# A grouped softmax over 285 MB: tiles of 384 rows for 256, a maximum ahead only within a tile, rows at a tile's ends scaled in halves

## The chip, the cores and the metric

One core of a Trainium2 chip. The metric is the device time of one execution, in microseconds; runs are repeated and the median is quoted.

## The reference, cut to what matters

```python
x: float32 [4, 4096, 4352]                 # 16384 rows of 17,408 bytes
x_g = x.reshape(B, N, 8, 544)              # eight groups in each row
x_g = x_g - x_g.max(axis=-1, keepdims=True)
exp = np.exp(x_g)
out = exp / exp.sum(axis=-1, keepdims=True)
```

285 MB come in and 285 MB go out. "A row" below means 128 rows of x, one on each partition: 2.2 MB, 128 such rows in all.

## The kernel before: the parts that matter

A ring of six buffers, each holding R = 2 rows per partition. SyncE issues the loads, each when the store that used its buffer is complete; GpSimd issues the stores (SyncE the last two). A load or a store is one transfer. In the trace it has 128 packets of R x 17,408 bytes (7936 of 34,816 bytes for GpSimd's 62 stores) and lands in 16 parts, so eight packets a part; a part is taken below for the share of one of the core's 16 DMA engines.

```python
# SyncE: loads
for t in range(nt):
    if t >= NT:
        nc.sync.wait_ge(stored[t % NT], 16 * (t // NT))
    nc.sync.dma_start(out=tile_in[:, :], in_=xt[t]).then_inc(landed[t % NT], 16)
    # ... the last tile is loaded row by row
# VectorE: one maximum ahead, all through
vector_max(0)
for s in range(S):
    vector_max(s + 1)     # waits for the next tile's load where s + 1 begins a tile
    vector_scale(s)       # reciprocal of the sums (waits for exp), then one multiply of 4352
# ScalarE: eight exps a row, one per group, each with its sum; the last one signals
```

Of the kernel before, what the change touches and what calls it, by code (L numbers as in the profile page):

```python
# [1 line left out]

# [5 lines left out]


@with_exitstack  # L10
def kernel(
    ctx: ExitStack,
    tc: tile.TileContext,
    x: bass.AP,
    out: bass.AP,
):
    nc = tc.nc
    G = 8
    P = 128
    R = 2  # L20
    NT = 6
    S = R * NT
    xf = x.flatten_outer_dims()
    of = out.flatten_outer_dims()
    N, D = xf.shape
    Dg = D // G
    nt = N // (P * R)
    nr = nt * R
    turns = (nr - 1) // S
    LAST = 2  # L30
    ring_turns = (nt - LAST) // NT
    steps = ring_turns * NT
    f32 = mybir.dt.float32
    X = mybir.AxisListType.X
    Exp = mybir.ActivationFunctionType.Exp
    xt = xf.rearrange("(t p r) d -> t p (r d)", p=P, r=R)
    ot = of.rearrange("(t p r) d -> t p (r d)", p=P, r=R)
    turn_out = of[:steps * P * R, :].rearrange("(u b p r) d -> u b p (r d)", b=NT, p=P, r=R)

    landed = [tc.alloc_semaphore(f"landed{b}") for b in range(NT)]  # L40
    stored = [tc.alloc_semaphore(f"stored{b}") for b in range(NT)]

    max_done = tc.alloc_semaphore("max_done")
    exp_done = tc.alloc_semaphore("exp_done")
    rec_done = tc.alloc_semaphore("rec_done")
    scaled = tc.alloc_semaphore("scaled")
    last_landed = tc.alloc_semaphore("last_landed")
    last_scaled = tc.alloc_semaphore("last_scaled")
    last_stored = tc.alloc_semaphore("last_stored")

    ctx.enter_context(tc.tile_critical(no_gpsimd_drain=True))  # L51
    bufs = [ctx.enter_context(nc.sbuf_tensor(f"xt{b}", [P, R * D], f32)) for b in range(NT)]
    mx = ctx.enter_context(nc.sbuf_tensor("mx", [P, S, G], f32))
    sm = ctx.enter_context(nc.sbuf_tensor("sm", [P, S, G], f32))
    rs = ctx.enter_context(nc.sbuf_tensor("rs", [P, S, G], f32))

    def take(engine, sem, n=1):
        engine.sem_inc(sem, -n).wait_op(sem, n, "sem-ge")  # L58

    def row(s):  # L60
        b, r = divmod(s, R)
        return bufs[b][:, r * D:(r + 1) * D].rearrange("p (g d) -> p g d", g=G)

    def vector_max(n):
        s = n % S
        i = nc.vector.reduce_max(out=mx[:, s, :], in_=row(s), axis=X, negate=True)  # L66
        if n == nr - 1:
            i.wait_op(last_landed, 16, "sem-ge")
        elif s % R == 0:
            i.wait_op(landed[s // R], 16, "sem-ge")  # L70
        i.then_inc(max_done, 1)

    def vector_scale(n):
        s = n % S
        nc.vector.reciprocal(out=rs[:, s, :], in_=sm[:, s, :]).wait_op(  # L75
            exp_done, s + 1, "sem-ge").then_inc(rec_done, 1)
        xr = row(s)
        nc.vector.tensor_tensor(  # L78
            out=xr,
            in0=xr,  # L80
            in1=rs[:, s, :].unsqueeze(2).to_broadcast([P, G, Dg]),
            op=mybir.AluOpType.mult,
        ).wait_op(rec_done, s + 1, "sem-ge").then_inc(
            scaled if n < (nt - LAST) * R else last_scaled, 1)

    def scalar_exp(s):
        xr = row(s)
        for g in range(G):
            i = nc.scalar.activation(  # L89
                out=xr[:, g, :],  # L90
                in_=xr[:, g, :],
                func=Exp,
                bias=mx[:, s, g:g + 1],
                scale=1.0,
                accum_out=sm[:, s, g:g + 1],
            )
            if g == 0:
                i.wait_op(max_done, s + 1, "sem-ge")
        i.then_inc(exp_done, 1)



    for t in range(nt):
        if t >= NT:
            nc.sync.wait_ge(stored[t % NT], 16 * (t // NT))
        tile_in = bufs[t % NT]
        if t < nt - 1:
            nc.sync.dma_start(out=tile_in[:, :], in_=xt[t]).then_inc(landed[t % NT], 16)  # L108
        else:
            for r in range(R):  # L110
                nc.sync.dma_start(
                    out=tile_in[:, r * D:(r + 1) * D], in_=xt[t, :, r * D:(r + 1) * D],
                ).then_inc(landed[t % NT] if r < R - 1 else last_landed, 16)
    for k in range(LAST):
        t = nt - LAST + k
        nc.sync.wait_ge(last_scaled, (k + 1) * R)
        nc.sync.dma_start(out=ot[t], in_=bufs[t % NT][:, :]).then_inc(last_stored, 16)
    nc.sync.wait_ge(last_stored, 16 * LAST)


    def store(t, target):
        take(nc.gpsimd, scaled, R)
        nc.gpsimd.dma_start(out=target, in_=bufs[t % NT][:, :]).then_inc(stored[t % NT], 16)  # L123

    with nc.gpsimd.Fori(0, ring_turns) as u:
        for t in range(NT):
            store(t, turn_out[u, t])
    for t in range(steps, nt - LAST):
        store(t, ot[t])
    for t in range(nt - NT, nt - LAST):  # L130
        nc.gpsimd.wait_ge(stored[t % NT], 16 * (t // NT + 1))
    nc.gpsimd.drain()

    nc.scalar.preload_act_table(Exp)  # L134
    with nc.Fori(0, turns, engines=OrderedEngineSet([nc.scalar.engine]),
                 head_slot={nc.scalar.engine: 0}):
        for s in range(S):
            scalar_exp(s)
        nc.scalar.sem_inc(max_done, -S)
    for n in range(turns * S, nr):  # L140
        scalar_exp(n % S)


    vector_max(0)
    with nc.vector.Fori(0, turns):
        for s in range(S):
            if s == S - 1:
                for b in range(NT):
                    nc.vector.sem_inc(landed[b], -16)
            vector_max(s + 1)  # L150
            vector_scale(s)
        nc.vector.sem_inc(exp_done, -S)
        nc.vector.sem_inc(rec_done, -S)
    for n in range(turns * S, nr):
        if n + 1 < nr:
            vector_max(n + 1)
        vector_scale(n)


# [1 line left out]
_INS = ['x']  # L161
_OUTS = [((4, 4096, 4352), 'float32')]


# [23 lines left out]
```

## Time and profile before

| | kernel before |
|---|---|
| median | 1327.84 us (1326.93 to 1328.22 over 4 runs) |
| span of the profile | 1326.6 us |
| VectorE busy | 1207.7 us, 91% |
| moved by DMA | 570.47 MB, 430 GB/s over the span |

Read it from the bottom up. 91% for VectorE looks like a bound, but the row of the DMA engines is full in every slice but the last, and the rate does not follow what the engines do: 433 GB/s from 4 to 40 us with VectorE busy for 24.2 of 36 us, and 433 from 330 to 1200 us with it busy for 797 of 870. The prediction below shows those lines. One view is worth reading with suspicion: the chain of waits puts 66% of the span on "another core or an unknown queue". Only one core runs, and SyncE's own waits name what it waited for (columns: us in total, times, longest):

```profile
SPq L108 <- DMA out_dram<-xt: 1213.4, 58, 62.2
```

SyncE is waiting for stores to free buffers nearly all the time: the DMA engines are what there is too little of.

### The profile page before, as it was taken

Reading aid. Unit: us, or ns where it says so; the run is one execution under the profiler, and the core shown is the slowest. Engines: PE = TensorE matmul, PEld = TensorE weight load, DVE = VectorE, ACT = ScalarE, POOL = GpSimd, SP = SyncE. Lnnn points to the kernel's source line nnn. Section 1 sums busy time; section 2 is a strip of 40 time slices with the busy share of each in tenths; the row PEclk is TensorE's granted clock in tenths of the full one; section 3 lists DMA queues with packets and bytes.
Section 4 is the critical chain, followed back from the end, with each engine's and each line's share of the span. In section 5 each row is a group of like instructions: output and inputs, shape, how many; then the busy total and the mean of one; then the engine's idle time right before and its main releaser. Section 6 shows DMA issues by size and latency. Waiting matters only on the chain.

```text
span 1326.6 us, 2968 instructions
## 1 busy us (share of the span) xinstructions
DVE 1207.7 (91%) x384; ACT 764.5 (58%) x2049; POOL 33.3 (3%) x66
## 2 busy tenths in 40 slices
DVE  5999999999889898898998989989889898898984
ACT  3666665656555565555655556556565565555661
POOL 0000000000000000000000000000000000000000
DMA  9999999999999999999999999999999999999998
GB/s 404 420 436 430 429 435 436 436 429 431 435 435 436 430 430 435 436 436 429 431 435 435 436 430 431 434 436 436 429 431 435 435 436 431 429 435 436 431 433 351
DMA packets 18581, 570.47 MB, mean 430 GB/s; under 512 B 2064, under 2 KB 2064, under 8 KB 2064
## 3 DMA queue, kind: packets, MB, share of 16 engines
q1 hardware_dynamic: 9648, 294.13, 51.5%
q0 software_dynamic: 8928, 276.30, 48.2%
q14 instruction: 5, 0.04, 0.0%
HBM read 285.21 MB, written 285.21 MB: 430 GB/s over the span
## 4 chain that ended last, share of the span: by engine, by line
another core or an unknown queue 66%; DMA 7%; DVE 3%; SPq 1%; ACT 0%; issue 0%; POOLq 0%
DMA out_dram<-xt 4%; DMA xt<-in_x_dram 3%; DVE xt L78 1%; DVE mx L66 1%; SPq L108 1%; ACT xt L89 0%; DVE rs L75 0%; POOLq L123 0%
## 5 line engine op out<-in xcount | busy, mean ns | idle before, releaser
L89 ACT ACTIVATE xt<-xt,mx 128x544 f32<-128x544 f32 x1024 | 751.3, 735 | 539.5 <-DVE mx L66 539.5
L66 DVE TENSOR_REDUCE mx<-xt 128x8 f32<-128x4352 f32 x128 | 599.1, 4681 | 95.3 <-DMA xt<-in_x_dram 95.3
L78 DVE TENSOR_TENSOR xt<-xt,rs 128x4352 f32<-128x4352 f32 x128 | 600.6, 4692 | 4.4
L89 ACT ACTIVATION_READ_ACCUMULATOR xt<-xt,mx 128x1 f32 x1024 | 191.2, 187 | 0.0
L123 POOL DMA_DIRECT2D out_dram<-xt x62 | 33.1, 533 | 1240.3 <-POOLq L58 1240.3
L75 DVE RECIPROCAL rs<-sm 128x8 f32<-128x8 f32 x128 | 24.7, 193 | 2.6 <-ACT xt L89 2.6
L134 ACT ACT_TABLE_LOAD x1 | 1.3, 1283 | 1.0 <-SPq L51 1.0
L172 POOL MEMSET const-float32-0.0<- 128x1 f32 x1 | 0.1, 98 | 0.4 <-issue 0.4
L172 POOL MEMSET const-bfloat16-1.0<- 128x1 bf16 x1 | 0.1, 101 | 0.0
L172 POOL MEMSET const-uint8-127<- 128x1 uint8 x1 | 0.1, 99 | 0.0
L172 POOL MEMSET const-float32-1.0<- 128x1 f32 x1 | 0.1, 98 | 0.0
## 6 DMA issues: line engine op xcount, KB each, us to landing
xt<-in_x_dram SPq DMA_DIRECT2D x63, 4352.0 KB, 41.1
out_dram<-xt POOLq DMA_DIRECT2D x62, 4352.0 KB, 51.5
out_dram<-xt SPq DMA_DIRECT2D x2, 4352.0 KB, 19.3
xt<-in_x_dram SPq DMA_DIRECT2D x2, 2176.0 KB, 43.5
```

The costliest lines, as they stand in the source:

```text
L66: i = nc.vector.reduce_max(out=mx[:, s, :], in_=row(s), axis=X, negate=True)
L75: nc.vector.reciprocal(out=rs[:, s, :], in_=sm[:, s, :]).wait_op(exp_done, s + 1, "sem-ge").then_inc(rec_done, 1)
L78: nc.vector.tensor_tensor(out=xr, in0=xr, in1=rs[:, s, :].unsqueeze(2).to_broadcast([P, G, Dg]), op=mybir.AluOpType.mult,).wait_op(rec_don ...
L89: i = nc.scalar.activation(out=xr[:, g, :], in_=xr[:, g, :], func=Exp, bias=mx[:, s, g:g + 1], scale=1.0, accum_out=sm[:, s, g:g + 1],)
L108: nc.sync.dma_start(out=tile_in[:, :], in_=xt[t]).then_inc(landed[t % NT], 16)
L123: nc.gpsimd.dma_start(out=target, in_=bufs[t % NT][:, :]).then_inc(stored[t % NT], 16)
L134: nc.scalar.preload_act_table(Exp)
L172: nc = _bacc.Bacc("TRN2", target_bir_lowering=False, num_devices=1)
```

## The change

Its intent: larger packets, fewer transfers, an earlier start, and a VectorE that finishes a tile, and so releases its store, without first waiting for the next load. To do that it keeps one maximum ahead inside a tile (two maxima stand before the first scaling, as before) but takes none of the next tile before a tile's last scaling. It scales a tile's first and last row in halves, so that the first multiply of such a row needs only half of its exps. The first tile is loaded row by row. 128 rows do not divide by 3, so the last tile has two rows. Cut to its core:

```diff
-    R = 2
-    NT = 6
+    R = 3
+    NT = 4
...
+    def vector_tile(t):
+        n = t * R
+        if sizes[t] == R:
+            vector_max(n)
+            for r in range(R):
+                if r + 1 < R:
+                    vector_max(n + r + 1)
+                vector_scale(n + r, 1 if 0 < r < R - 1 else H)   # H = 2 parts
+        else:                                                     # the last tile, two rows
+            for r in range(sizes[t]):
+                vector_max(n + r)
+                vector_scale(n + r, H)
...
-        i.then_inc(exp_done, 1)
+            if (g + 1) % Gh == 0:          # after four and after eight exps
+                i.then_inc(exp_done, 1)
...
-            vector_max(s + 1)
-            vector_scale(s)
+            vector_tile(t)
```

More of the change, by code (lines that the diff above doesn't have):

```diff
@@ L26 @@
     Dg = D // G
-    nt = N // (P * R)
-    nr = nt * R
-    turns = (nr - 1) // S
+    nr = N // P
+    sizes = nr // R * [R]
+    if nr % R:
+        sizes.append(nr % R)
+    nt = len(sizes)
+    turns = (nt - 1) // NT
+    H = 2
+    Gh = G // H
     LAST = 2
@@ L35, with tile_of @@
     Exp = mybir.ActivationFunctionType.Exp
-    xt = xf.rearrange("(t p r) d -> t p (r d)", p=P, r=R)
-    ot = of.rearrange("(t p r) d -> t p (r d)", p=P, r=R)
+    def tile_of(af, t):
+        lo = t * P * R
+        return af[lo:lo + P * sizes[t], :].rearrange("(p r) d -> p (r d)", p=P)
     turn_out = of[:steps * P * R, :].rearrange("(u b p r) d -> u b p (r d)", b=NT, p=P, r=R)
@@ L46 @@
     scaled = tc.alloc_semaphore("scaled")
-    last_landed = tc.alloc_semaphore("last_landed")
+    first_landed = [tc.alloc_semaphore(f"first_landed{r}") for r in range(1, R)]
+    last_landed = [tc.alloc_semaphore(f"last_landed{r}") for r in range(1, sizes[-1])]
     last_scaled = tc.alloc_semaphore("last_scaled")
@@ L66, in vector_max, with vector_scale @@
         i = nc.vector.reduce_max(out=mx[:, s, :], in_=row(s), axis=X, negate=True)
-        if n == nr - 1:
-            i.wait_op(last_landed, 16, "sem-ge")
-        elif s % R == 0:
+        r = n % R
+        if r == 0:
             i.wait_op(landed[s // R], 16, "sem-ge")
+        elif n < R:
+            i.wait_op(first_landed[r - 1], 16, "sem-ge")
+        elif n // R == nt - 1:
+            i.wait_op(last_landed[r - 1], 16, "sem-ge")
         i.then_inc(max_done, 1)
-    def vector_scale(n):
+    recs = 0
+    def vector_scale(n, parts):
+        nonlocal recs
         s = n % S
-        nc.vector.reciprocal(out=rs[:, s, :], in_=sm[:, s, :]).wait_op(
-            exp_done, s + 1, "sem-ge").then_inc(rec_done, 1)
-        xr = row(s)
-        nc.vector.tensor_tensor(
-            out=xr,
-            in0=xr,
-            in1=rs[:, s, :].unsqueeze(2).to_broadcast([P, G, Dg]),
-            op=mybir.AluOpType.mult,
-        ).wait_op(rec_done, s + 1, "sem-ge").then_inc(
-            scaled if n < (nt - LAST) * R else last_scaled, 1)
+        for k in range(parts):
+            g = slice(k * G // parts, (k + 1) * G // parts)
+            nc.vector.reciprocal(out=rs[:, s, g], in_=sm[:, s, g]).wait_op(
+                exp_done, H * s + (k + 1) * H // parts, "sem-ge").then_inc(rec_done, 1)
+            recs += 1
+            xr = row(s)[:, g, :]
+            i = nc.vector.tensor_tensor(
+                out=xr,
+                in0=xr,
+                in1=rs[:, s, g].unsqueeze(2).to_broadcast([P, G // parts, Dg]),
+                op=mybir.AluOpType.mult,
+            ).wait_op(rec_done, recs, "sem-ge")
+        i.then_inc(scaled if n // R < nt - LAST else last_scaled, 1)
+    def vector_tile(t):
[10 more added lines that the diff above has]
+                vector_scale(n + r, H)
     def scalar_exp(s):
@@ L105 @@
             nc.sync.wait_ge(stored[t % NT], 16 * (t // NT))
-        tile_in = bufs[t % NT]
-        if t < nt - 1:
-            nc.sync.dma_start(out=tile_in[:, :], in_=xt[t]).then_inc(landed[t % NT], 16)
-        else:
-            for r in range(R):
-                nc.sync.dma_start(
-                    out=tile_in[:, r * D:(r + 1) * D], in_=xt[t, :, r * D:(r + 1) * D],
-                ).then_inc(landed[t % NT] if r < R - 1 else last_landed, 16)
-    for k in range(LAST):
-        t = nt - LAST + k
-        nc.sync.wait_ge(last_scaled, (k + 1) * R)
-        nc.sync.dma_start(out=ot[t], in_=bufs[t % NT][:, :]).then_inc(last_stored, 16)
+        tile_in, source = bufs[t % NT], tile_of(xf, t)
+        if 0 < t < nt - 1:
+            nc.sync.dma_start(out=tile_in[:, :], in_=source).then_inc(landed[t % NT], 16)
+            continue
+        others = last_landed if t else first_landed
+        for r in range(sizes[t]):
+            nc.sync.dma_start(
+                out=tile_in[:, r * D:(r + 1) * D], in_=source[:, r * D:(r + 1) * D],
+            ).then_inc(others[r - 1] if r else landed[t % NT], 16)
+    rows = 0
+    for t in range(nt - LAST, nt):
+        rows += sizes[t]
+        nc.sync.wait_ge(last_scaled, rows)
+        nc.sync.dma_start(
+            out=tile_of(of, t), in_=bufs[t % NT][:, :sizes[t] * D]).then_inc(last_stored, 16)
     nc.sync.wait_ge(last_stored, 16 * LAST)
@@ L128 @@
     for t in range(steps, nt - LAST):
-        store(t, ot[t])
+        store(t, tile_of(of, t))
     for t in range(nt - NT, nt - LAST):
@@ L141 @@
         scalar_exp(n % S)
-    vector_max(0)
     with nc.vector.Fori(0, turns):
-        for s in range(S):
-            if s == S - 1:
-                for b in range(NT):
-                    nc.vector.sem_inc(landed[b], -16)
-            vector_max(s + 1)
-            vector_scale(s)
-        nc.vector.sem_inc(exp_done, -S)
-        nc.vector.sem_inc(rec_done, -S)
-    for n in range(turns * S, nr):
-        if n + 1 < nr:
-            vector_max(n + 1)
-        vector_scale(n)
+        for t in range(NT):
+            vector_tile(t)
+        for b in range(NT):
+            nc.vector.sem_inc(landed[b], -16)
+        nc.vector.sem_inc(exp_done, -H * S)
+        nc.vector.sem_inc(rec_done, -recs)
+    recs = 0
+    for t in range(turns * NT, nt):
+        vector_tile(t)
 _INS = ['x']
```

## The prediction

The start of the first store at 43.0 is the estimate; in the records of packets the first store's first packet begins at 44.85 in the kernel before, 4.65 us after the issue. That 433 GB/s is a wall rests on the constant rate of the flat stretches alone.

Two readings of the trace belong to the text as well. That the queues take turns: from 330 to 1200 us of the kernel before, with packets of one size in both, loads and stores move 217 GB/s each; from 1265 to 1274, where stores in packets of 34,816 bytes run beside loads in packets of 17,408, they move 291 and loads 142, so about as many packets of each (75 and 73). And that one part drifts behind the other 15 is measured; that it is the same DMA engine's each time ("the slow engine", here and below) is inferred, as the trace does not number the engines.

> **What bounds the kernel now.** I read the page first (busy shares, slices, queues), then the waits, then a table of windows, the timeline of the last 60 us, and last the trace's records of single packets and of the landings of each transfer's 16 parts.
>
> The page: VectorE (DVE) is busy for 91%, but the DMA row is at 9 in all but the last slice.
>
> ```profile
> DVE 1207.7 (91%) x384; ACT 764.5 (58%) x2049; POOL 33.3 (3%) x66
> DMA  9999999999999999999999999999999999999998
> DMA packets 18581, 570.47 MB, mean 430 GB/s; under 512 B 2064, under 2 KB 2064, under 8 KB 2064
> xt<-in_x_dram SPq DMA_DIRECT2D x63, 4352.0 KB, 41.1
> out_dram<-xt POOLq DMA_DIRECT2D x62, 4352.0 KB, 51.5
> ```
>
> The windows say the same by stage (columns: busy us of each engine, clock, DMA share, GB/s). Outside the first 4 us, the stretch where the first store begins (40 to 46) and the last 5 us, the transfers move 433 GB/s, whatever the engines do.
>
> ```profile
> 2.00:4.00 2.00, 0.00 (x0) 0.32 (x1) 0.00 (x0) 1.00 1.05 283
> 4.00:40.00 36.00, 24.22 (x8) 17.26 (x47) 0.00 (x0) 1.00 1.00 433
> 40.00:46.00 6.00, 5.97 (x3) 2.53 (x7) 0.67 (x1) 1.00 1.02 371
> 330.00:1200.00 870.00, 797.10 (x253) 505.15 (x1357) 22.32 (x42) 1.00 1.00 433
> 1320.00:1322.00 2.00, 0.00 (x0) 0.00 (x0) 0.00 (x0) 1.00 0.21 87
> 1322.00:1326.60 4.60, 0.00 (x0) 0.00 (x0) 0.00 (x0) 1.00 0.04 15
> ```
>
> 570.47 MB at 433.5 GB/s (my sharper value for the flat stretches, from the packets) is 1316 us of the 1326.6. So the kernel is a transfer of x in and out at a constant rate, and only 10 us are anything else: 2.3 us before the first byte, 1 us at the first store, some 5 us at the end, 1.4 us after the last landing. VectorE's waits confirm that it is the one that is fed:
>
> ```profile
> DVE mx L66 <- DMA xt<-in_x_dram: 95.3, 50, 14.3
> ```
>
> The end matters most. The landings of the 16 parts of each store show one part drifting behind: the last lies 0.1 us behind the last but one early on, 4.0 us for the store that lands at 1294.5. The final two stores are complete at 1315.1 and 1325.2; the first part of the final one is there at 1321.5. From 1315.1 to 1325.2 is 10.1 us, which is eight packets of 1.29 us, one part's share of a 4.456 MB store. So the slow DMA engine went from the one store into the other without a gap: it is busy from 3 us to the end. The kernel before ends when the slowest DMA engine has done its share, and VectorE's last work (ending 1309.96) is already hidden.
>
> ```profile
> 1294.32 4.69 DVE L66 TENSOR_REDUCE mx<-xt 128x8 f32<-128x4352 f32 x1 [2.64 <-DMA xt<-in_x_dram]
> 1305.04 0.20 DVE L75 RECIPROCAL rs<-sm 128x8 f32<-128x8 f32 x1 [1.20 <-ACT xt L89]
> 1305.27 4.69 DVE L78 TENSOR_TENSOR xt<-xt,rs 128x4352 f32<-128x4352 f32 x1
> 1291.71 18.63 SPq L117 DMA_DIRECT2D out_dram<-xt  x2
> ```
>
> [...]
>
> **The change part by part.**
> Bytes: unchanged. Buffers: 4 of 3 rows for 6 of 2, the same memory.
>
> Packets: a packet is one partition's run: 52,224 bytes for 34,816. Packet records last 648 ns at 17,408 bytes and 1288 ns at 34,816: 640 ns per 17,408 bytes and 8 ns fixed. As records overlap a little, the period is 1285 ns, so the fixed cost is nearer 5. Per DMA engine there were 64 x 16 = 1024 packets; there will be 41 x 16 + (24 + 8) for the first tile + (16 + 8) for the last = 712. Saved: 312 x 5 = 1.6 us. The slow engine's mean packet is 1321/1024 = 1290 ns, 10 over the 1280 of its bytes; if all of that is per packet, 3.2 us. I take 2.2.
>
> Start: rows of the first tile land singly at about 9.1, 14.3 and 19.5 (5.2 us each at full rate), so VectorE starts 5 us sooner. Its first tile is 28.6 us of work with a gap, ending at 38.7 against 39.4: the first store starts 0.7 us sooner. Worth nothing, as loads fill the DMA engines until 65 us either way.
>
> VectorE's load: a row cost 9.43 us (the step from one maximum to the next). A row in halves costs 2 x (0.23 + 2.42 - 0.08) = 5.14 for 4.84, 0.30 more. Three rows with two halved: 28.3 + 0.6 = 28.9 us, against a DMA period of 2 x 15.44 = 30.9 us. So the kernel stays bound by transfers, with 2 us of slack per tile. Two maxima ahead keep ScalarE off the path: exp takes 5.9 us per row, and VectorE always has that much between.
>
> Not waiting for the next load: that wait was 1.7 us a tile in the steady state, on an engine with slack. Worth nothing there.
>
> End: here it costs. The state of the queues when the last full tile (41) lands, at L, decides. All loads of the first four tiles, 61.8 us of DMA time from 3.2, share the DMA engines with stores from about 43.0[...]. Shared half and half, tile 3 lands at 65 + (65 - 43) = 87.0; store 0 ends at 43 + 30.9 = 73.9, store 1 at 104.8, 17.8 us after the landing of tile 3. Both queues then always hold work and take turns, so the offset stays: at a landing, the store two tiles back has 17.8/2 = 8.9 us of DMA time left. (The same sum for the kernel before gives a landing 1 us after a store's end; measured 1.1 to 1.5.)
> So at L there are left: load of the last tile 10.3, rest of store 39 8.9, stores 40 and 41 15.4 each, the final store 10.3: 60.4 us. With every DMA engine busy the end would be as before less the saving, so L = 1325.2 - 2.2 - 60.4 = 1262.6.
> VectorE after L: tile 41, 28.95; the last tile has no second maximum ahead, so each of its two rows takes maximum 4.7 + half an exp 3.1 + halves 5.2 = 13.0: 25.9 in all. Finished at L + 54.85. The final store lands 12.2 after that (before: 1309.96 to 1321.5 for the first part, plus the usual 0.7). The other stores are done by L + 50.1, so the DMA engines stand idle for about 6 us. End: 1262.6 + 54.85 + 12.2 + 1.4 = 1331.0 of span, and 1.2 more in the timed runs: 1332.2.
> So: -2.2 (packets), +6.5 (a tail that VectorE sets), other parts 0: about +4 us.
>
> **The rivals.**
> First: the tail stays hidden. If store 39 has its whole 15.4 us left at L (the kernel before had two whole stores waiting at the like point), there is no idle time, and only the packets count: about 1325.5. Against it: the offset that I worked out; for it: it rests on one estimate of the first store's start, each us of which moves it by 1.
> Second: the slow engine's delay is per packet[...], and larger packets cure more than I count: 3.2 for 2.2, or with a flattened drift 4 us: 1329 to 1330.
> Third: four buffers starve a queue. A cycle of four tiles is 123.6 us; VectorE holds a buffer 29, a load and a store need 31 each at half rate, so 32 us of slack remain, over the 4 to 7 us by which the DMA engines lie apart. I expect no gap. If VectorE became the bound, its sum 9.1 + 42 x 28.9 + 25.9 + 12 + 1.4 = 1262 is far below the wall, so this too costs nothing by itself; a gap of 0.3 us a tile would make 1345.
> Fourth: finishing without the wait gives much. It would need VectorE on the path; nothing in the profile says so, and the wall of 1316 + 3 + 2 leaves at most 0.5%.
>
> **Range and chances.** Between the first rival's 1325.5 and my sum 1332, with some weight on the second: 1331, and 8 in 10 within 1325.5 to 1335. No part reaches 2% (26 us) either way: faster 0.01, same 0.98, slower 0.01.
>
> **What would show it.** In the windows of the changed kernel, 433 to 434 GB/s in the steady state, packets of 52,224 bytes lasting about 1928 ns; reduce waits for loads of about 2 us on nearly each tile from the ninth; halves of 2.42 us. At the end, VectorE without a wait for some 55 us, then a final store issued when the DMA has been quiet for about 6 us, and its 16 parts landing within 1 us of each other. I am wrong if the final store follows the one before without a gap, if the DMA row dips in mid-run, or if the rate of the steady state moves by more than 0.5%.

## The result, and the profile after

| | before | after |
|---|---|---|
| median of 4 runs | 1327.84 us | 1333.72 us |
| range | 1326.93 to 1328.22 | 1332.18 to 1334.00 |
| span of the profile | 1326.6 us | 1332.2 us |
| VectorE busy | 1207.7 us | 1225.6 us |

The ratio is 1.0043, with a 95% interval of 1.0025 to 1.0060: a small loss, the same within 2%. (Ratios here and below are the mean time of one kernel's fast runs over that of the other's fast runs of the same rounds, so not quite the ratio of the quoted medians; in the experiments the profiled run is in the median but not in the ratio. Executions over 1.5% slower than the fastest of the same kernel are left out of the means.)

The page of the changed kernel, the lines that answer to those of before:

```profile
DVE 1225.6 (92%) x556; ACT 759.9 (57%) x2049; POOL 22.1 (2%) x45
DMA  9999999999999999999999999999999999999996
DMA packets 12821, 570.47 MB, mean 428 GB/s; under 512 B 1424, under 2 KB 1424, under 8 KB 1424
xt<-in_x_dram SPq DMA_DIRECT2D x41, 6528.0 KB, 45.6
out_dram<-xt POOLq DMA_DIRECT2D x41, 6528.0 KB, 47.6
```

The same bytes in a third fewer packets, and a row of nines until the last slice, which fell from 8 to 6. The steady state is not slower: over the stretch from 100 to 1240 us the changed kernel moves 434 GB/s for 433. What was lost was lost in the last slice. Its windows, before and after (columns: window, its length, busy us of VectorE, ScalarE and GpSimd with their instructions, clock, DMA share, GB/s). First the kernel before:

```profile
1308.00:1312.00 4.00, 1.96 (x1) 0.00 (x0) 0.00 (x0) 1.00 0.71 305
1312.00:1316.00 4.00, 0.00 (x0) 0.00 (x0) 0.00 (x0) 1.00 0.98 418
1316.00:1320.00 4.00, 0.00 (x0) 0.00 (x0) 0.00 (x0) 1.00 1.19 514
1320.00:1324.00 4.00, 0.00 (x0) 0.00 (x0) 0.00 (x0) 1.00 0.14 61
```

Then the changed kernel:

```profile
1304.00:1308.00 4.00, 4.00 (x2) 0.00 (x0) 0.00 (x0) 1.00 0.97 418
1308.00:1312.00 4.00, 2.41 (x1) 1.56 (x5) 0.00 (x0) 1.00 0.06 26
1312.00:1316.00 4.00, 2.46 (x2) 4.00 (x12) 0.00 (x0) 1.00 0.00 0
1316.00:1320.00 4.00, 2.75 (x3) 0.41 (x2) 0.00 (x0) 1.00 0.14 61
1320.00:1324.00 4.00, 0.00 (x0) 0.00 (x0) 0.00 (x0) 1.00 1.16 496
```

(A packet is booked whole into the window that it begins in, so neighbouring windows can stand a little over or under the true rate.) Before, transfers run on while VectorE finishes and after. After, all but the slowest DMA engine stand still from 1310 to 1319 (the last but one of the second last store's 16 parts lands at 1310.01, the last at 1312.71) while VectorE and ScalarE work, and the final store follows. The timeline of VectorE says what it was doing (columns: start us, us, instruction, and in brackets the idle time before it):

```profile
1263.66 9.28 DVE L76 TENSOR_REDUCE mx<-xt 128x8 f32<-128x4352 f32 x2 [1.97 <-DMA xt<-in_x_dram]
...
1292.47 4.68 DVE L76 TENSOR_REDUCE mx<-xt 128x8 f32<-128x4352 f32 x1
1300.25 0.18 DVE L94 RECIPROCAL rs<-sm 128x4 f32<-128x4 f32 x1 [3.10 <-ACT xt L123]
1300.47 2.42 DVE L98 TENSOR_TENSOR xt<-xt,rs 128x2176 f32<-128x2176 f32 x1
1303.18 0.18 DVE L94 RECIPROCAL rs<-sm 128x4 f32<-128x4 f32 x1 [0.29 <-ACT xt L123]
1303.39 2.42 DVE L98 TENSOR_TENSOR xt<-xt,rs 128x2176 f32<-128x2176 f32 x1
1305.73 4.68 DVE L76 TENSOR_REDUCE mx<-xt 128x8 f32<-128x4352 f32 x1
1313.51 0.18 DVE L94 RECIPROCAL rs<-sm 128x4 f32<-128x4 f32 x1 [3.10 <-ACT xt L123]
...
1316.65 2.42 DVE L98 TENSOR_TENSOR xt<-xt,rs 128x2176 f32<-128x2176 f32 x1
```

The last full tile lands at 1263.64 and VectorE needs until 1319.07, 55.4 us. In the two rows of the last tile it waits 3.10 us each for half an exp. From the landings of the 16 parts of each transfer: the second last store is complete at 1312.71, the final one at 1330.80.

### The profile page after: what moved, and what is told of

It is laid out like the page before. It is cut to its first block, busy times and chain, and to the rows that moved or that the text cites. A ratio compares the mean times of both kernels' runs of the same rounds, so it can differ in the third digit from the quotient of the medians.

```text
span 1332.2 us, 3018 instructions
## 1 busy us (share of the span) xinstructions
DVE 1225.6 (92%) x556; ACT 759.9 (57%) x2049; POOL 22.1 (2%) x45
## 5 line engine op out<-in xcount | busy, mean ns | idle before, releaser
L76 DVE TENSOR_REDUCE mx<-xt 128x8 f32<-128x4352 f32 x128 | 595.6, 4679 | 79.4 <-DMA xt<-in_x_dram 79.4
L98 DVE TENSOR_TENSOR xt<-xt,rs 128x2176 f32<-128x2176 f32 (+1 forms) x214 | 614.1, 2869 | 7.3
L94 DVE RECIPROCAL rs<-sm 128x4 f32<-128x4 f32 (+1 forms) x214 | 37.2, 174 | 6.8 <-ACT xt L123 6.8
L161 POOL DMA_DIRECT2D out_dram<-xt x41 | 21.9, 535 | 1240.4 <-POOLq L68 1240.4
## 6 DMA issues: line engine op xcount, KB each, us to landing
out_dram<-xt SPq DMA_DIRECT2D x1, 4352.0 KB, 11.7
```

The lines of the kernel that those rows point to most:

```text
L76: i = nc.vector.reduce_max(out=mx[:, s, :], in_=row(s), axis=X, negate=True)
L94: nc.vector.reciprocal(out=rs[:, s, g], in_=sm[:, s, g]).wait_op(exp_done, H * s + (k + 1) * H // parts, "sem-ge").then_inc(rec_done, 1)
L98: i = nc.vector.tensor_tensor(out=xr, in0=xr, in1=rs[:, s, g].unsqueeze(2).to_broadcast([P, G // parts, Dg]), op=mybir.AluOpType.mult,).wa ...
L161: nc.gpsimd.dma_start(out=target, in_=bufs[t % NT][:, :]).then_inc(stored[t % NT], 16)
```

## The experiments

Twelve kernels ran, with the kernel before beside them on the same chip each time (medians 1327.9 to 1328.0). All gave correct results. Ratios are to the kernel before.

| run | median | range | ratio |
|---|---|---|---|
| e7_one_pad | 1328.05 | 1327.66 to 1328.22 | 1.0001 |
| e7_two_pads | 1332.17 | 1332.02 to 1332.69 | 1.0033 |
| e1_single_rows | 1335.51 | 1334.85 to 1335.74 | 1.0057 |
| e8_small_pads | 1335.83 | 1335.64 to 1338.01 | 1.0065 |
| e9_large_pads | 1358.19 | 1358.05 to 1358.79 | 1.0228 |
| e3_whole_rows | 1361.80 | 1361.67 to 1362.23 | 1.0256 |
| e5_row_stores | 1329.77 | 1327.06 to 1332.85 | 1.0007 |
| e4_order_before (five fast runs) | 1333.82 | 1331.26 to 1351.17 | 1.0081 |
| e6_order_and_row_stores | 1330.11 | 1328.79 to 1332.05 | 1.0018 |
| e10_late_first_store | 1334.82 | 1330.04 to 1340.38 | 1.0042 |
| e2_first_tile_whole | 1340.29 | 1329.20 to 1344.14 | 1.0068 |
| e11_order_late_first_store | 1328.71 | 1327.59 to 1339.95 | 1.0027 |

### Is the tail of the kernel before really hidden?

In the kernel before, idle work on VectorE ahead of its very last scaling (the result is thrown away):

```diff
+        if n == nr - 1:
+            for k in range(1):        # 2 in the second kernel
+                nc.vector.reduce_max(out=pad[:, k, :], in_=row(s - 2), axis=X)
         nc.vector.reciprocal(...)
```

> The kernel before with one idle maximum of 4.7 us on VectorE ahead of its very last scaling, where it waits 1.2 us for exp anyway, so that its end comes 3.5 us later. My theory (the slow DMA engine has work until 1315, some 4 us past the last store's issue): 0 to 1 us slower. Rival (VectorE's end is on the path, as the chain of waits has it): 3.5 us slower.

> The kernel before with two idle maxima there: VectorE ends 8.2 us later. My theory: past the slack of 3 to 5 us, so 3 to 5 us slower. Rival: 8.2 us slower.

VectorE's last scaling, with one pad and then with two:

```profile
1308.58 4.69 DVE L82 TENSOR_TENSOR xt<-xt,rs 128x4352 f32<-128x4352 f32 x1
1313.23 4.69 DVE L82 TENSOR_TENSOR xt<-xt,rs 128x4352 f32<-128x4352 f32 x1
```

Measured: VectorE ends at 1313.27 and 1317.92, for 1309.96; the span stays at 1326.6 with one and becomes 1331.0 with two. The first 3.3 us cost nothing; of the next 4.65 us, 4.4 show. So the slack was there and is about as large as the expectation put it: VectorE could be 3 to 4 us later, no more. The rival, VectorE's end on the path, would have given 3.5 and 8.2.

### What does a packet cost?

The kernel before with `R = 1`, `NT = 12` in place of 2 and 6: packets of half the size, twice as many, the same memory, and a tail that is still hidden.

> The kernel before with tiles of 128 rows and twelve buffers: packets of 17,408 bytes, 2048 a DMA engine for 1024, in a kernel whose tail is hidden. My theory (a packet costs 5 ns beside its bytes, some more on the slow engine): 1024 x 5 to 10 = 5 to 10 us slower, 1333 to 1338, with a steady rate of 432 or a little less for 433.4 GB/s. Rival (packet size doesn't matter, the saving in the changed kernel came from elsewhere): 1327 to 1329.

Measured: 7.6 us slower by the medians, for 1016 more packets on each DMA engine: 7.5 ns a packet. (2048 for 1032: the kernel before loads its last tile row by row, 8 packets that the expectation and the prediction left out. The tail did stay hidden: VectorE ends at 1320.2, and the slowest engine has the store before the last done at 1326.7 and the last at 1332.4.) In the stretch from 100 to 1240 us the rates of the three packet sizes, one row each of windows from the single-row kernel, the kernel before and the changed kernel, stand in order:

```profile
100.00:1240.00 1140.00, 1051.56 (x334) 661.10 (x1775) 58.98 (x111) 1.00 1.01 431
```

```profile
100.00:1240.00 1140.00, 1061.17 (x339) 671.77 (x1803) 29.75 (x56) 1.00 1.00 433
```

```profile
100.00:1240.00 1140.00, 1065.94 (x483) 660.25 (x1783) 19.66 (x37) 1.00 1.00 434
```

From this an estimate of the saving in the changed kernel: 320 packets fewer (712 for 1032) at 7.5 ns are 2.4 us.

### How much slack has VectorE in the changed kernel?

```diff
         if sizes[t] == R:
+            nc.vector.reduce_max(out=pad[:, t % NT, :], in_=row(n % S)[:, 0:2, :], axis=X,
+                ).wait_op(landed[t % NT], 16, "sem-ge")     # 0:4 in the second kernel
```

> The changed kernel with an idle maximum over two groups of a row (1.2 us) on VectorE per tile of 384 rows, 50 us in all. My theory: within the slack of 1.7 to 2 us a tile, so only the one in the tail shows: 1 to 2 us slower than the changed kernel, 1334 to 1336. Rival (VectorE, busy for 92%, is the bound): up to 50 us slower.

> The same over four groups (2.3 us a tile, 98 us in all). My theory: past the slack, so VectorE becomes the bound, at 31.1 us a tile from its start: 1355 to 1362. Rival (still hidden): 1336.

Measured: 54 us of added work cost 2.1 us by the medians (1335.83 for 1333.72), although VectorE was then busy for 96% of the span. Twice as much cost 24.5. The waits of the two kernels say why. With the small pads VectorE still waits for loads at 31 tiles, with the large ones only for the first:

```profile
DVE pad L111 <- DMA xt<-in_x_dram: 31.7, 31, 9.2
```

```profile
DVE pad L111 <- DMA xt<-in_x_dram: 9.9, 1, 9.9
```

So the changed kernel's VectorE has some 2 us of slack a tile and is not the bound of its steady state, whatever "92% busy" suggests.

### Undoing the halves

```diff
-                vector_scale(n + r, 1 if 0 < r < R - 1 else H)
+                vector_scale(n + r, 1)
```

and likewise in the last tile.

> The changed kernel without halves: every row is scaled at once, order otherwise as changed. My theory: VectorE does 0.6 us a tile less, hidden in the steady state; in the last tile each of two rows waits 6 us for its exp in place of 3.1, and saves the cost of a half (0.3): 2 x 2.6 more, less 0.6 for tile 41: 4 to 5 us slower than the changed kernel (1337 to 1339). Rival (halves cost VectorE time that shows): faster.

Measured: 28 us slower, and both theories missed it. One tile of the steady state shows what I had left out:

```profile
635.96 4.68 DVE L76 TENSOR_REDUCE mx<-xt 128x8 f32<-128x4352 f32 x1
642.07 0.20 DVE L94 RECIPROCAL rs<-sm 128x8 f32<-128x8 f32 x1 [1.44 <-ACT xt L123]
...
657.63 0.20 DVE L94 RECIPROCAL rs<-sm 128x8 f32<-128x8 f32 x1 [1.19 <-ACT xt L123]
657.87 4.69 DVE L98 TENSOR_TENSOR xt<-xt,rs 128x4352 f32<-128x4352 f32 x1
662.48 9.27 DVE L76 TENSOR_REDUCE mx<-xt 128x8 f32<-128x4352 f32 x2
```

An exp of a whole row takes 6.0 us, and VectorE has only one other instruction of 4.6 to put in front of the first scaling of a tile, and one of 4.6 in front of the last. It waits 1.44 + 1.19 = 2.6 us a tile. With 28.3 us of work that is 31 us a tile, just over what the DMA engines need (30.9, from the bytes of a tile in and out at 433 GB/s): the waits for loads are gone (9.7 us in two waits, for 79.4 in 37) and VectorE has become the bound. So the halves are not a cost of 0.6 us a tile; they cost 0.5 (in the changed kernel's trace a row in halves takes 5.09 us from its first reciprocal to the next maximum, a row at once 4.83 to the next reciprocal) and take away 2.6, and without them an order that stops at a tile's end would not keep up.

### Shortening the tail: stores row by row

```diff
-        nc.sync.wait_ge(last_scaled, rows)          # the whole tile
-        nc.sync.dma_start(out=tile_of(of, t), in_=bufs[t % NT][:, :sizes[t] * D])
+        for r in range(sizes[t]):                   # each row as it is scaled, last two tiles
+            rows += 1
+            nc.sync.wait_ge(last_scaled, rows)
+            nc.sync.dma_start(out=tile_of(of, t)[:, r * D:(r + 1) * D], ...)
```

> The changed kernel, whose last two tiles are stored row by row as each row is scaled. My theory: the DMA engines get work in what was their idle time, and after VectorE's end only one row is left (5.2 us for 10.3): 5 us faster, 1328 to 1329. Rival (the end is set by a fixed latency of the last store, not by its size): no change.

Measured: 1329.77 in the median, 4.0 us below the changed kernel and just above the range of the expectation, and 1327.06 at best. The intervals of the ratios to the kernel before do not meet: 0.9994 to 1.0020, for 1.0025 to 1.0060 of the changed kernel. The rival (a fixed latency at the end) is out. In its profile the last row lands 6.6 us after VectorE's end (1323.25 to 1329.84), for 11.7 with a store of two rows. The runs scatter over 6 us, where the kernel before has 1.6; of that below.

### VectorE's order of before, on the large tiles

`vector_max(s + 1); vector_scale(s, 1)` all through, across tiles, in place of `vector_tile`. This undoes the halves as well.

> The changed kernel with VectorE's order of before: one maximum ahead all through, across tiles, each row scaled at once; tiles stay 384 rows, four buffers. My theory: the steady state is the same, but VectorE needs only some 49 us after the landing of the last full tile (five maxima, five scalings, a wait of 1.2) for 55.4, so the DMA engines hardly idle: 5 to 7 us faster than the changed kernel, 1327 to 1329, at or up to 1 us below the kernel before (the packet saving of 2.2 less a rest of idle time). Rival (four large buffers themselves cost the time): still 1332 to 1334.

> Tiles of 384 rows, VectorE's order of before, and the last two tiles stored row by row. My theory: no DMA idle time is left in the tail, so the packet saving of 2.2 us comes out: 1325 to 1326.5, faster than both kernels by a little. Rival (the small packets of five row stores and their issues give the saving back): 1327 to 1329.

Measured: 1331.26 to 1351.17 without row stores (a sixth run, 1351.74, is slow, though its clock is 1.00 like that of all the others), 1328.79 to 1332.05 with them. Both expectations were missed: the median of 1333.82 lies where the rival had it (1332 to 1334), that of e6, 1330.11, above theory and rival. The first expectation had an error of arithmetic: with this order one scaling of tile 40 is still to do when tile 41 lands, so VectorE's work after that landing is five maxima and six scalings, 53.4 us in its trace, not 49; only 2 us are gained in the tail. That does not explain the scatter up to 1351, nor why the packet saving does not come out with row stores added.

### Moving the first store

If the offset between loads and stores, set by the first store, decides what work the tail has left, then delaying that store should make the kernel faster. Two ways, and one with the order of before:

```diff
+    # SyncE, after the load of tile 2: a small transfer behind it in the same queue
+                nc.sync.dma_start(out=pad[:, :], in_=source[:, :128]).then_inc(go, 16)
+    # GpSimd, ahead of its first store
+    nc.gpsimd.wait_ge(go, 16)
```

> The changed kernel, whose first store is held back until the load of its third tile has landed (near 59 us in place of 40). My theory (the offset between loads and stores, fixed by the first store, decides how much DMA work is left for the tail): stores then end just ahead of the load two tiles on, so the store two tiles back still has some 15 us of DMA time left when the last full tile lands, for 7 to 9; that landing comes about 6 us sooner, VectorE's 55 us after it are unchanged, and the kernel is 4 to 7 us faster than the changed one (1327 to 1329), though it only delays something. Rival (the tail is VectorE's alone, or the start matters): no change, or slower by the delay.

> Tiles of 384 rows, VectorE's order of before, and the first store held back until the third tile has landed. My theory: the same end as with row stores, no DMA idle time in the tail: 1325 to 1326.5. Rival: 1327 to 1329 as with the order alone, or slower.

The other way is to load the first tile by one transfer, as before (`if t < nt - 1` in place of `if 0 < t < nt - 1`):

> The changed kernel, whose first tile is loaded by one transfer in place of three. My theory: VectorE starts some 10 us later, at 19.5, and the first store comes some 8 us later, near 48; no DMA work is lost, as loads fill the DMA engines until 65. But the first store's delay moves the offset of stores against loads by 16 us, up to where it can go, so the tail has up to 6 us more DMA work left: 4 to 7 us faster than the changed kernel, 1327 to 1329. Rival (an earlier start is a gain, or is worth nothing): slower by up to 10 us, or the same 1333.

Measured: the first store is issued at 49.9 to 51.9 us, for 39.5 in the changed kernel; the times scattered. The theory missed all three times: the medians lie where the rivals had them (no gain, or 1327 to 1329 for e11). What speaks for the theory is e11 against e4, which has the same order without the delay: in the profiles the last full tile lands at 1259.85 for 1265.25, and the spans are 1327.2 and 1331.7; but another run of e11 took 1339.95. In the profiles of e10 and e2 that tile lands at 1270.20 and 1273.99, later than the changed kernel's 1263.64 and not some 6 us sooner; these profiles are of their slowest runs. Their best runs, 1330.04 and 1329.20, are below every run of the changed kernel, their medians above it. The changed kernel's own four runs lie within 1.8 us. So a second effect costs 0 to 15 us from run to run in these.

The traces show what comes with it. When a store completes, the load of its buffer is issued; "lead" below is how long that load then lies in its queue before the load ahead of it has its first part landed, that is, before it could begin. "Stretched" are packets of 100 to 1240 us that took 30 ns or more longer than the median packet (worked out from the records of single packets; e1 and the two runs of e7 have 5 to 28, at most 2 of them of loads):

```
                 lead, first   median   stretched packets   (of loads)   sum, us
                 after 100 us
kernel before        19.9       18.3           20                0           1.2
changed kernel       10.8       10.8            8                0           0.6
e5                   10.5        5.5           87               61          14.6
e8                   10.4        6.1           74               50          11.7
e4                    5.7        5.8           99               93          14.9
e11                   6.0        5.5           50               44           6.5
e6                    4.7        3.8           99               96          14.8
e10                   6.4        2.1          147              131          34.2
e2                    3.2        2.1          431              396         112.1
e3                    7.7       -2.1          223              176          91.1
e9                    6.9       -2.0          297              233         120.0
```

Short leads and stretched packets, most of them packets of loads, stand together. That the short lead is the cause is not shown, and e5 and e8 speak against it. e5's program is the changed kernel's up to the last two tiles, and its lead starts at nearly the same 10.5 us; yet from 100 to 231 us, with the lead still above 9, 12 of its packets are stretched, 8 of them of loads (e8: 18 and 15; the changed kernel: 3 and none). Its lead then shrinks to 4.8 by 1222 us, while the slowest part of a store falls from 0.7 to 6.3 us behind the median part. A load is issued when the slowest part of a store is complete (in the kernel before, stores whose last parts land at 87.16 and 190.01 us are followed by loads issued at 87.18 and 190.02), so a late engine shortens the lead by as much as it is late. A short lead is thus in part what stretched packets leave behind. In the other direction, e11 starts at 6.0 and has only 3 stretched packets of loads from 100 to 600 us.

The view of transfers for the stretch from 300 to 1240 us shows the shorter lead too (last number: median us from issue to landing); the changed kernel, then e10:

```profile
xt<-in_x_dram SPq DMA_DIRECT2D x30, 6528.0 KB, 46.0
```

```profile
xt<-in_x_dram SPq DMA_DIRECT2D x30, 6528.0 KB, 38.9
```

The sum, spread over 16 DMA engines, is only 2.1 us each for e10, but the delay does not fall evenly: for the stores that end from 1100 to 1250 us, the slowest part lies 19.8 us behind the median part in e10's profile and 19.6 in e2's, for 1.5 in the changed kernel and 4.0 in the kernel before. A store is complete with its slowest part, so a late engine is paid in full. At the last store of GpSimd's queue the same lag is 13.3 and 12.7 us, for 3.1 in the changed kernel; but the kernel before has 9.5 there with almost nothing stretched, so a lag has other sources too. The third rival of the prediction (four buffers too few for two queues) does not show in the changed kernel's own trace and four runs. As e5 repeats its steady state and has stretched packets, the changed kernel is not shown to be free of them.

Three things stay open. What stretches a packet, the traces do not say: a short lead, the chip (e5 ran on another one than e8; the changed kernel's is not recorded) or something else. That the delay on one DMA engine is the sum of those stretched packets is argued from their coming together, not shown: the records do not name a packet's engine. And the profiles are of one run each, those of e2, e5 and e10 of the slowest.

## Why the prediction was right

Its steps, in its order, against the profile of the changed kernel:

| step | predicted | measured |
|---|---|---|
| packets | 2.2 us saved | 2.2, worked out: other stores done at 1312.71, plus 10.3 for the final one is 1323.0, for 1325.2 |
| offset of stores against loads | tile 3 at 87.0, store 1 at 104.8 | first parts at 87.39 and 104.70 |
| landing of the last full tile, L | 1262.6 | 1263.64 |
| VectorE after L | 54.85 us | 55.4 |
| other stores done | L + 50.1 | L + 49.1 |
| final store after VectorE | 12.2 us | 11.7 |
| span | 1331.0 | 1332.2 |
| timed run | 1332.2 by the sum; 1331.0 stated | 1333.72 |

- What bounds the kernel: right. The steady state is a wall of 433 to 434 GB/s in both, and in e8 54 us of extra work for VectorE cost 2.
- Its signs came: packets of 1928 ns, nothing moved from 1312.7 to 1319.1, and the 16 parts of the final store within 0.2 us of each other.
- The tail: right, and the whole of the loss. The slow DMA engine has its other stores done at 1312.71 and gets the final one near 1320; these 7 to 8 us, less 2.2 for the packets, are the 5.6 us between the spans. The rival that the tail stays hidden is out; the experiments with idle maxima show that before, 3 to 4 us of slack were all there was.
- Two terms were a little off. Each row of the last tile waits once more, 0.29 us, for the second half of its exps: 0.6 us of VectorE's 55.4. And store 39 had 7.7 us of work left at L instead of 8.9: it is complete 10.3 us after L (1273.95), and it shares the DMA engines with a load in single rows, whose packets are a third of its own. The 7.7 is an estimate: four of its packets of 1.928 us and four of the load's of 0.648 make up the 10.3. (By their records, packets that begin in that stretch move 2.92 MB of stores and 1.39 of loads on all engines.) For the last parts the offset had shrunk from 17.3 us at tile 3 to 15.4 near the end, as the last part falls behind a little more in loads than in stores: behind the last but one by 0.4 us for tile 3's load and 2.8 for the one that lands at 1232.78, and by 0.0 and 1.0 for the stores two tiles back, which land at 107.38 and 1248.20. For the first parts it is still 17.3.
- From the sum of 1332.2 I stated 1331.0, leaning towards the rivals that gave less; the sum was nearer. Of the 1.5 us that the sum lacked, 0.4 are the step from span to timed run (1.2 taken, 1.6 measured). The sum of packets left out the 8 of the last tile's single rows before: 320 are saved, not 312, which is under 0.1 us.
- "Worth nothing" for the earlier start was right for the start itself, but incomplete: in e2 loading the first tile whole, which moves VectorE's start and the first store, leaves loads a lead of 3.2 us from the start, for 10.8.
- What the prediction said of the halves (0.6 us a tile, hidden) was about true of their cost (0.5 measured) and missed their use: without them VectorE is the bound (e3). "Two maxima ahead keep ScalarE off the path" is the step that hid this: behind a tile's first maximum stands one more, 4.6 us, which covers half a row's exps (3.0) and not a row's (6.0). It takes the halves to keep ScalarE off the path.
- It did not see what the parts do for each other. Ending a tile without waiting for the next load releases stores sooner, and with four buffers that leaves loads 10.8 us of lead at the start; it is 5.7 in e4, which undoes order and halves, and 7.7 in e3, which undoes the halves alone.

None of the twelve beats the kernel before: its tail was already hidden, so what is to be had is the packets' 2.2 us, and the versions that keep it either idle at the end or scatter. The best runs of e5 and e11, 1327.06 and 1327.59, are within the range of the kernel before.

## What to carry to other kernels

When the DMA row is full from end to end, as it was here (54 us of added work for VectorE cost 2.1), ask of a change only what it does to the bytes, the packets and the two ends: follow the slowest DMA engine to its last packet, and compare the work still queued when the last full tile lands with the compute that follows that landing. Larger tiles saved little here (7.5 ns a packet by e1, an estimated 2.4 us in all) and lengthened exactly that compute (55.4 us after the landing). Fewer, larger buffers also left less time between a load's issue and its start (10.8 us for 19.9). Whether that is what made the variants here scatter is open; look at the scatter of runs as well as the median, and repeat a profile before you read a cause from one.
